# Neighbourhood attention: two places for pieces in a step, first scores among the projections, right output halves among the last steps

## The chip, the cores and the metric

The kernel runs on one core of a Trainium2 chip. Its time is that of one execution on the device, in microseconds (us). The engines of a core run beside each other, each in its own fixed order, and wait for each other by semaphores: TensorE (PE) multiplies and transposes, VectorE (DVE), ScalarE (ACT) and GpSimd (POOL) work on tiles, and SyncE (SP) issues most of the DMA transfers. PE writes to banks of PSUM, which the other engines read and so release.

## What is computed

Two layers of a diffusion backbone on 128 prompt tokens and 1024 latent tokens of width 1024. Layer 0 projects each token into a convolution module and eight heads of attention, each with a SiLU gate, and projects the joined results back; layer 1 is a pooling mixer. The change lies in the attention of layer 0 and in the start of its output projection.

```python
q = rms_norm(q, q_norm); k = rms_norm(k, k_norm)          # 8 heads of 64
# prompt: plain softmax attention of 128 tokens
# latent: each query sees a window of 8 rows x 16 columns, and all 128 cached keys
s_win = q . k_window * 64**-0.5 + rpb      # blocks of 16 columns: 8 rows x 32 keys, masked
s_ctx = q . k_ctx * 64**-0.5
p = softmax(concat(s_win, s_ctx)); y_att = p . concat(v_window, v_ctx)
z = concat(y_conv * silu(ga), y_att * silu(gb));  y = x + gate * (z @ w_out)
```

## The kernel before

All products are made in float32 by splitting both factors into a high and a low part and adding three matmuls. Projections run in chains of 24 matmuls (L232) for a group of 384 tokens (three groups, g) and 128 output columns; the last stage of them, `p_ga`, makes the gate of the convolution, four chains for each group. Ahead of the attention it calls `attention_ahead(g)`, which lays down the bias of the first pair of heads, the first pair's q and k (`prep`) and its values.

The attention is a list of 16 steps: four pairs of heads, two halves of the tokens (hf), two pairs of column blocks (j0). The functions in a step are

- `scores`: twelve matmuls (L877) into four banks of the kind "mm". Four times DVE adds the bias and takes the maximum (L885), ACT takes the exponential (L892), DVE the reciprocal (L896), and POOL scales p (L898). `p` stands in tiles of the kind `whi`, which also hold split weights.
- `turn`: four transposes of p (L904) into a bank of the kind "tp" or "cv" (there are two of each), four turns a step. ACT copies three of the banks to `pt` (L1033, L1038), DVE the last (L1039).
- `values`: 32 matmuls (L913) into a "cv" bank, and DVE multiplies the gate in (L924).
- pieces. `prep` of the next pair has five: two halves of q (L813), two halves of k (L820), each four transposes whose high part ACT writes (L804) and whose low part DVE writes (L805); and `rest` (L832 to L834), three transposes with two copies to `qc` on ACT, the high part of the cached keys on ACT (L840), the low part on DVE and two copies on POOL. `prompt_attention` has four: scores (L938) with DVE's maxima and scale (L940, L941) and two exps on ACT (L943); the scaling by POOL (L948); two transposes and a copy (L953, L954); the values (L959).

The order on PE, ACT and DVE in the attention is the order of the code, written out in `attention_steps` by hand; the order on POOL and SP is set by a scheduler when the kernel is built and is then as fixed. In the loop for s the scores of step s + 1 come first, then the values of step s - 1, then the turns of step s. The pieces come at the end of a step:

```python
            prompt[i]()
            for piece in pieces[2 * i : 2 * i + 2]:
                later.append(piece())
```

i is s % 4. All of them take "cv" banks (the prompt's parts also "tp"), and DVE's part of a piece, `later`, runs at the start of the next step. The first scores, of steps 0 and 1, come after the last projection.

After the attention `out0` projects nine tiles of 128 tokens: `out_right` and `out_left` are 24 matmuls each (L1101, L1094), for 512 of 1024 columns. Right weights are loaded and split by `load_right` (L1063 on SP, two buffers; L1073 on POOL, L1074 on DVE) among the last four steps. Left weights are two units, loaded at L204, split by ACT (L186) and DVE (L187); the layer's gates come by four loads (L408), x by y loads (L1118), z is split by L1085 and L1086.

Of the kernel before, what the change touches and what calls it, by code (L numbers as in the profile page):

```python
# [46 lines left out]
def _body(tc, nc, A, O, const, wp, arena, tmpp, smp, psp):  # L47
# [736 lines left out]
    def v_load(pr):  # L784
        vw = {}
        for jj in range(2):
            t = slot(VS[pr % 2][jj], name="vw")[:, :1280].rearrange("p (x c) -> p x c", c=P)
# [9 lines left out]
    def prep(pr):  # L797
# [9 lines left out]
        def q_half(i):  # L807
            if i == 0:
                st["q"] = [slot(x, F32R, "q")[:, :D] for x in QS[pr % 2]]
            b = bank("cv")  # L810
# [6 lines left out]
        def k_half(i):  # L817
            b = bank("cv")
            for t in range(4):
                te.transpose(out=b[:, t * P : (t + 1) * P], in_=qk_at(4 * i + t, pr)[:, P : 2 * P], identity=ident)  # L820
            if i == 0:

                st["k"] = [slot(x, F32R, "k") if x is not None else gr_tile(F32R)[:, :SLOT] for x in KS[pr % 2]]
# [3 lines left out]
        def rest():  # L827
# [3 lines left out]
            b = bank("cv")  # L831
# [3 lines left out]
            se.activation(qc[:, 0:P], b[:, 0:P], AF.Copy, scale=qn8)  # L835
            se.activation(qc[:, P : 2 * P], b[:, P : 2 * P], AF.Copy, scale=kn)
# [13 lines left out]
        return [lambda: q_half(0), lambda: q_half(1), lambda: k_half(0), lambda: k_half(1), rest]  # L850
# [11 lines left out]
    def scores(step, mem=None):  # L862
# [7 lines left out]
        def matmuls(i):  # L870
# [7 lines left out]
            if mem is not None:  # L878
                ps.append(mem[:, i * 1024 : (i + 1) * 1024].rearrange("p (e k) -> p e k", e=2))
            else:  # L880
                ps.append(wp.tile([P, 2, 512], F32, tag="whi", bufs=4, name=nm("p")))
# [47 lines left out]
    def prompt_attention(pr):  # L929
# [5 lines left out]
        def first():  # L935
# [9 lines left out]
        def second():  # L945
            ve.reciprocal(st[:, 6:8], st[:, 4:6])
            for e in range(2):
                gp.tensor_scalar(pp[:, e * P : (e + 1) * P], pp[:, e * P : (e + 1) * P], st[:, 6 + e : 7 + e], 0.0, ALU.mult, ALU.add)  # L948

        def third():  # L950
            tb = bank("tp")
            for e in range(2):
                te.transpose(out=tb[:, e * P : (e + 1) * P], in_=pp[:, e * P : (e + 1) * P], identity=ident)  # L953
            se.copy(pp[:, 2 * P : 4 * P], tb[:, : 2 * P])  # L954

        def fourth():
            ob = bank("cv")
# [6 lines left out]
            ve.tensor_tensor(zv, ob[:, :P], zv, ALU.mult)  # L964

        return first, second, third, fourth
# [3 lines left out]
    def attention_ahead(g):  # L970
# [4 lines left out]
        elif g == 1:  # L975
            for piece in prep(0):
                piece()()
            with tc.issue_after(last["ck"]):
                hold["V"] = v_load(0)
        else:  # L980
            bias_init(1)
            bias_load(0, 1)

    def attention():
        nonlocal gr
        first = hold["S"] = scores(STEPS[0], gr_tile())
        for i in range(2):
            first[0](i)
            for e in range(2):
                first[1](i, e)  # L990
            first[2](i)
# [3 lines left out]
        gr = gr_tile()  # L995

    def attention_steps():


        n = len(STEPS)  # L1000
        sc_, vw, pts = {0: hold["S"]}, {0: hold["V"]}, {}
        pieces, later, right = [], [], None
        for s in range(n + 1):
            i, pr = s % 4, s // 4
            while later:
                later.pop(0)()
            nxt = None
            if s + 1 < n:
# [3 lines left out]
                nxt[1](0, 0)  # L1012
                nxt[1](0, 1)
                nxt[1](1, 0)
# [12 lines left out]
            ps = sc_.pop(s)[3]  # L1027
            pt = pts[s] = [wp.tile([P, 2, 512], F32, tag="wlo", bufs=4, name=nm("pt")) for _ in range(2)]
# [5 lines left out]
            if nxt:  # L1034
                nxt[1](1, 1)
            tb = bank("tp")
# [5 lines left out]
            prompt[i]()  # L1042
            for piece in pieces[2 * i : 2 * i + 2]:
                later.append(piece())
            if i == 2 and pr < 3:
                vw[pr + 1] = v_load(pr + 1)
            if pr == 3:
                if i == 0:
                    right = load_right(0, (13, 15, 17, 2, 3, 4))
                hold["R"] = next(right)  # L1050


    def load_right(l, ids, ahead=2):
# [11 lines left out]
        for k0 in range(0, 2 * ahead, 2):  # L1065
            load(k0)
        for k0 in range(0, 8, 2):
# [11 lines left out]
    def zsplit(zt, t, ids):  # L1079
# [3 lines left out]
        for kh in range(2):  # L1083
            src = zt[g, kh][:, :, a : a + P]
            se.copy(hi[:, 4 * kh : 4 * kh + 4, :], src)  # L1085
            ve.tensor_tensor(lo[:, 4 * kh : 4 * kh + 4, :], src, f(hi[:, 4 * kh : 4 * kh + 4, :]), ALU.subtract)  # L1086
        return hi, lo

# [23 lines left out]

    def out0(WL, WR, gate):
        zt = {(g, kh): (zc, za)[kh][g] for g in range(3) for kh in range(2)}
        xn = []
        for t in range(9):
            y = slot((0, 1, 8, 9)[t % 4], name="y")[:, :D]
            sy.dma_start(y, x_src(t))  # L1118
            zs = zsplit(zt, t, ((5, 16), (6, 7))[t % 2])
            c = 1 if t == 8 else 0  # L1120
            add_gated(y, out_right(zs, WR), 1, gate[c, 1])
# [158 lines left out]
    def go_out0():  # L1280
        gate = load_gates(0)
        out0(hold["L0"] + hold["L1"], hold["R"], gate)
# [65 lines left out]
```

## Time and profile before

| | us |
|---|---|
| median of 3 runs | 996.78 (994.22 to 997.67) |
| profiled execution | 996.42 |
| its span in the profile | 994.6 |
| PE busy in the span | 951.6 |
| DVE, ACT, POOL busy | 599.2, 408.3, 366.9 |

The profile is of one execution, and its span is 1.8 us shorter than the execution's time. A bracket behind a row of the timeline is idle time of that engine ahead of the row and what ended it. Ends of matmuls are modelled, so the distance of two starts tells more than a matmul's own length.

### The profile page before, as it was taken

Reading aid. Unit: us, or ns where it says so; the run is one execution under the profiler, and the core shown is the slowest. Engines: PE = TensorE matmul, PEld = TensorE weight load, DVE = VectorE, ACT = ScalarE, POOL = GpSimd, SP = SyncE. Lnnn points to the kernel's source line nnn. Section 1 sums busy time; section 2 is a strip of 40 time slices with the busy share of each in tenths; the row PEclk is TensorE's granted clock in tenths of the full one; section 3 lists DMA queues with packets and bytes.
Section 4 is the critical chain, followed back from the end, with each engine's and each line's share of the span. In section 5 each row is a group of like instructions: output and inputs, shape, how many; then the busy total and the mean of one; then the engine's idle time right before and its main releaser. Section 6 shows DMA issues by size and latency. Waiting matters only on the chain.

```text
span 994.6 us, 16662 instructions
## 1 busy us (share of the span) xinstructions
PE 951.6 (96%) x6388; PEld 865.3 (87%) x6388; DVE 599.2 (60%) x1231; ACT 408.3 (41%) x827; POOL 366.9 (37%) x485
## 2 busy tenths in 40 slices
PE   5888999999999999998898899999999999999998
PEld 3686988899999999986677788889999999998887
DVE  3567999999763344456677556475435545585332
ACT  3375666765411244247777423335212222231010
POOL 2264888998743301024445245351000000004322
PEclk9998999999999999999999999999999999999999
DMA  9969654226111111133433612151101111133311
GB/s 299 337 196 288 233 172 146 87 86 234 46 46 46 46 43 43 37 85 111 114 103 97 212 65 105 44 200 48 41 29 43 53 43 54 64 106 101 132 64 65
DMA packets 87531, 108.54 MB, mean 109 GB/s; under 512 B 10700, under 2 KB 73036, under 8 KB 87339
## 3 DMA queue, kind: packets, MB, share of 16 engines
q1 hardware_dynamic: 82539, 95.93, 30.5%
q0 software_dynamic: 2576, 9.18, 2.4%
q10 hardware_dynamic: 2336, 2.36, 0.7%
q8 instruction: 50, 0.82, 0.3%
q14 instruction: 30, 0.25, 0.1%
HBM read 94.64 MB, written 21.57 MB: 117 GB/s over the span
## 4 chain that ended last, share of the span: by engine, by line
PE 83%; DMA 5%; DVE 4%; ACT 3%; SPq 3%; issue 2%; POOL 1%; DVEq 0%; POOLq 0%; ACTq 0%
PE mm L232 39%; PE mm L239 16%; PE mm L1101 10%; PE mm L1094 9%; PE mm L1246 2%; PE tp L342 2%; ACT p L892 2%; SPq L757 2%; DMA raw<-in_w_out 1%; DVE p L885 1%; DMA bias<-texp 1%; PE mm L877 1%; DMA wad<-in_w_ada 1%; DMA raw<-in_w_in 1%; PE tp L904 1%
## 5 line engine op out<-in xcount | busy, mean ns | idle before, releaser
L232 PE MATMUL mm<-h,whi 128*128 128x384 f32 x1536 | 399.0, 339 | 2.7 <-ACT whi L186 1.8
L232 PEld LDWEIGHTS mm<-h,whi 128*128 128x128 f32 x1536 | 278.1, 189 | 10.0 <-ACT gr L474 2.6
L232 PE MATMUL mm<-h,wlo 128*128 128x384 f32 x768 | 258.7, 338 | 0.3 <-DVE wlo L187 0.3
L476 POOL TENSOR_TENSOR zc<-zc,gr 128x384 f32<-128x384 f32 x138 | 150.5, 1092 | 30.9 <-ACT gr L474 21.9
L239 PE MATMUL mm<-whi,h 128*128 128x256 f32 x864 | 157.1, 284 | 0.0
L232 PEld LDWEIGHTS mm<-h,wlo 128*128 128x128 f32 x768 | 145.4, 189 | 1.3 <-issue 0.7
L239 PEld LDWEIGHTS mm<-whi,h 128*128 128x128 f32 x864 | 135.1, 192 | 3.9 <-ACT gr L474 2.6
L239 PE MATMUL mm<-wlo,h 128*128 128x256 f32 x432 | 122.2, 283 | 0.0
L187 DVE TENSOR_TENSOR wlo<-raw,whi 128x1024 fp32r<-128x1024 f32 (+1 forms) x56 | 69.3, 1237 | 55.0 <-ACT whi L186 54.7
L487 DVE SCALAR_TENSOR_TENSOR cv<-u,convw,cv 128x384 f32<-128x384 f32 (+2 forms) x208 | 95.0, 511 | 0.9
L1094 PE MATMUL mm<-whi,zs 128*128 128x512 f32 (+1 forms) x304 | 92.8, 379 | 2.0 <-ACT whi L186 2.0
L1101 PE MATMUL mm<-wrh,zs 128*128 128x512 f32 x288 | 92.4, 391 | 0.4 <-POOL wrh L1073 0.4
L186 ACT CAST whi<-raw 128x1024 fp32r<-128x1024 f32 (+1 forms) x56 | 56.9, 1017 | 70.3 <-PE mm L232 23.6
L239 PEld LDWEIGHTS mm<-wlo,h 128*128 128x128 f32 x432 | 82.9, 192 | 0.0
L1108 POOL TENSOR_TENSOR y<-y,og 128x512 f32<-128x512 f32 x34 | 48.7, 1434 | 86.6 <-DVE og L1106 83.4
L474 ACT ACTIVATE gr<-u,convw 128x384 f32<-128x384 f32 (+2 forms) x128 | 64.3, 531 | 30.8 <-POOL zc L476 30.3
L1094 PEld LDWEIGHTS mm<-whi,zs 128*128 128x128 f32 x304 | 56.0, 188 | 12.7 <-ACT whi L186 2.2
L1101 PEld LDWEIGHTS mm<-wrh,zs 128*128 128x128 f32 x288 | 53.9, 188 | 11.9 <-POOL wrh L1073 0.8
L898 POOL TENSOR_SCALAR p<-p,st 128x512 f32<-128x512 f32 x60 | 44.3, 752 | 53.0 <-DVE st L896 45.3
L1106 DVE TENSOR_TENSOR og<-mm,gr 128x512 f32<-128x512 f32 x34 | 23.3, 687 | 57.7 <-PE mm L1101 33.4
L456 ACT ACTIVATE th<-mm 128x384 f32<-128x384 f32 x48 | 23.5, 489 | 83.1 <-PE mm L232 83.0
L1094 PE MATMUL mm<-wlo,zs 128*128 128x512 f32 (+1 forms) x152 | 57.3, 378 | 0.0
(216 smaller groups left out, 1380.2 us busy)
## 6 DMA issues: line engine op xcount, KB each, us to landing
raw<-in_w_in SPq DMA_DIRECT2D x28, 512.0 KB
wad<-in_w_ada SPq DMA_DIRECT2D x16, 768.0 KB
wada<-in_w_ada SPq DMA_DIRECT2D x16, 512.0 KB
raw<-in_w_in SPq DMA_DIRECT2D x32, 256.0 KB
raw<-in_w_out SPq DMA_DIRECT2D x16, 512.0 KB
vw<-vwin SPq DMA_DIRECT2D x8, 640.0 KB
y0scr<-y POOLq DMA_DIRECT2D x9, 512.0 KB, 3.2
y<-y0scr SPq DMA_DIRECT2D x9, 512.0 KB
```

Of the source, the lines that this page charges most:

```text
L186: se.copy(hi[:, :n], raw[:, :n])
L187: ve.tensor_tensor(lo[:, :n], raw[:, :n], f(hi[:, :n]), ALU.subtract)
L232: te.matmul(out, wsl(units, a, k, c0, P), hsl(hs, b, k, g), start=(k == 0 and i == 0), stop=(k == nk - 1 and i == 2))
L239: te.matmul(out, hsl(hs, p, k, g, a, P), wsl(units, q, k, 0, 256), start=(k == 0 and i == 0), stop=(k == 7 and i == 2))
L456: se.activation(th[:, :n], ps, AF.Tanh, scale=0.5)
L474: se.activation(pr[:, o : o + n], src, AF.Copy, scale=w)
L476: gp.tensor_tensor(z, z, pr, ALU.add)
L487: ve.scalar_tensor_tensor(zp if k == 30 else acc, src, convw[:, c, k : k + 1], zp if k == NPTS[c] else acc, ALU.mult, ALU.add)
L898: gp.tensor_scalar(ps[i][:, e, :], ps[i][:, e, :], st[:, 4 + e : 5 + e], 0.0, ALU.mult, ALU.add)
L1094: te.matmul(b[:, c0 : c0 + n], zs[p][:, k, :], WL[k // 2][q][:, k % 2, c0 : c0 + n], start=(k == 0 and i == 0), stop=(k == 7 and i == 2))
L1101: te.matmul(b, zs[p][:, k, :], WR[q][k // 3][:, k % 3, :], start=(k == 0 and i == 0), stop=(k == 7 and i == 2))
L1108: gp.tensor_tensor(yv, yv, t, ALU.add)
```

## The change

Three parts. First, the scores of step 0 are made in `p_ga`, ahead of the last projection chain (g = 2, i = 2); their p is in `whi` tiles instead of a tile of its own. The bias of the second half, the values of even pairs and the keys of odd pairs get other slots; the second bias is laid down one group earlier.

Second, each step has two places for pieces: a, with a "cv" bank, between the next step's scores and the values, and b, with a "tp" bank, ahead of the last turn. The place a piece gets:

| i | a | b |
|---|---|---|
| 0 | q, first half | q, second half |
| 1 | k, first half | k, second half |
| 2 | rest | prompt: scores |
| 3 | prompt: transposes | prompt: values |

DVE's part of a piece runs after the four reduces of the same step. The prompt's scaling joins its first piece, so there are three. `rest` copies to `qc` on DVE instead of ACT, and so does the prompt's copy. In the last pair, which has no `prep`, the prompt's three pieces stand at a in steps 12, 13 and 14.

Third, the right weights start one step earlier; the gates' loads and the first two y loads come in step 13, the raw loads of the first left unit and a part of z's split in step 14, the rest of the split of two tiles in step 15. `out_right` of tile 0 stands in step 15 between the values and the turns, that of tile 1 behind them, ahead of the last values.

```diff
+                if g == 2 and i == 2:
+                    first_scores()
             attention_ahead(g)
...
-    BS = ((0, 1), (8, 9))
+    BS = ((0, 1), (6, 7))
     QS = ((2, 3), (10, 11))
-    KS = ((4, 5), (None, 12))
-    VS = ((6, 7), (14, 16))
+    KS = ((4, 5), (9, 12))
+    VS = ((None, 8), (14, 16))
...
-            se.activation(qc[:, 0:P], b[:, 0:P], AF.Copy, scale=qn8)
-            se.activation(qc[:, P : 2 * P], b[:, P : 2 * P], AF.Copy, scale=kn)
...
+                ve.tensor_scalar(qc[:, 0:P], b[:, 0:P], qn8, None, ALU.mult)
+                ve.tensor_scalar(qc[:, P : 2 * P], b[:, P : 2 * P], kn, None, ALU.mult)
...
+    def first_scores():
+
+        mm, ex, norm, ps = hold["S"] = scores(STEPS[0])
+        for i in range(2):
+            mm(i)
+            for e in range(2):
+                ex(i, e)
+            norm(i)
...
+                ab = ([*prompt, None], [None] * 4) if last_ else ((pieces[0], pieces[2], pieces[4], prompt[1]), (pieces[1], pieces[3], prompt[0], prompt[2]))
+            if s == n - 2:
+                zs_part(0, 0)
+            if s == n - 1:
+                zs_part(0, 1)
+                zs_part(1, 0)
+                zs_part(1, 1)
+            if s == n:
+                out0_ahead(1)
+                units[L0_AT] = [split(*r) for r in raws[L0_AT]]
+            if nxt:
+                nxt[1](0, 0)
+            a = ab[0][i]("cv") if s < n and ab[0][i] else None
             gate = values(STEPS[s - 1], pts.pop(s - 1), vw[STEPS[s - 1][0]]) if s else None
+            if nxt:
+                nxt[1](0, 1)
+                nxt[1](1, 0)
+            if a:
+                a()
             if nxt:
                 nxt[2](0)
             if gate:
                 gate()
+            if s == n - 1:
+                out0_ahead(0)
...
+            b = ab[1][i]("tp") if ab[1][i] else None
             tb = bank("tp")
             turn(tb, ps[1][:, 1, :])
...
-            if pr == 3:
-                if i == 0:
-                    right = load_right(0, (13, 15, 17, 2, 3, 4))
+            if n - 6 <= s < n - 1:
                 hold["R"] = next(right)
+            if s == n - 3:
+                gr = gr_tile()
+                hold["gate"] = load_gates(0)
+                y_of(0)
+                y_of(1)
+            if s == n - 2:
+                raws[L0_AT] = load_raw(items[L0_AT][0])
```

On PE, around the prompt's transposes of the first pair, before, at the end of a third step (`tp` and `cv` are banks, `p` scaled scores, `pp` the prompt's p, the numbers are buffers):

```order
L904 MATMUL tp_5244<-ident,p_5093 128x128 x4
L904 MATMUL tp_5245<-ident,p_5093 128x128 x4
L904 MATMUL cv_5246<-ident,p_5105 128x128 x4
L904 MATMUL tp_5262<-ident,p_5105 128x128 x4
L953 MATMUL tp_5272<-ident,pp_5025 128x128 x2
L832 MATMUL cv_5278<-ident,qk_2995 128x128
L833 MATMUL cv_5278<-ident,qk_2995 128x128
L834 MATMUL cv_5278<-ident,qc_5276 128x128
L877 MATMUL mm_5292<-gr_5172,q_5069 128x512
```

And now, in the fourth step, behind the scores of the step that follows:

```order
L879 MATMUL mm_5302<-k_5107,q_5027 128x512
L954 MATMUL cv_5314<-ident,pp_5023 128x128 x2
L912 MATMUL cv_5317<-pt_5243,gr_4831 64x128 x8
L912 MATMUL cv_5317<-pt_5244,gr_4831 64x128 x8
L903 MATMUL tp_5344<-ident,p_5180 128x128 x4
L903 MATMUL tp_5345<-ident,p_5180 128x128 x4
L903 MATMUL cv_5346<-ident,p_5192 128x128 x4
L960 MATMUL tp_5362<-pp_5023,VP 64x128 x2
L903 MATMUL tp_5365<-ident,p_5192 128x128 x4
```

The transposes (L953, now L954) have gone from behind the turns of a third step to ahead of the values of a fourth, with the prompt's values (L960) ahead of the last turn of the same step.

On ACT in the scores of step 13, made in step 12, before (`p_6191` and `p_6203` are the two tiles of these scores, `pp_6210` is the last prompt's p):

```order
L892 ACTIVATE p_6191,st_6192<-p_6191,st_6192 128x512 x2
L892 ACTIVATE p_6203,st_6204<-p_6203,st_6204 128x512
L1033 COPY pt_6234<-tp_6236 128x512
L1033 COPY pt_6234<-tp_6237 128x512
L892 ACTIVATE p_6203,st_6204<-p_6203,st_6204 128x512
L1038 COPY pt_6235<-cv_6238 128x512
L943 ACTIVATE pp_6210,st_6211<-cv_6264,st_6211 128x128
L943 ACTIVATE pp_6210,st_6211<-tp_6265,st_6211 128x128
```

And now:

```order
L891 ACTIVATE p_6208,st_6209<-p_6208,st_6209 128x512
L942 ACTIVATE pp_6224,st_6225<-cv_6227,st_6225 128x128
L942 ACTIVATE pp_6224,st_6225<-tp_6228,st_6225 128x128
L891 ACTIVATE p_6208,st_6209<-p_6208,st_6209 128x512
L891 ACTIVATE p_6220,st_6221<-p_6220,st_6221 128x512
L1055 COPY pt_6263<-tp_6265 128x512
L1055 COPY pt_6263<-tp_6266 128x512
L891 ACTIVATE p_6220,st_6221<-p_6220,st_6221 128x512
L1061 COPY pt_6264<-cv_6267 128x512
```

The prompt's two exps (L943, now L942) have moved from the end of the step to a place between the first two of the four exps.

On POOL in the last steps, before (`wrh` are the high parts of right weights):

```order
L898 TENSOR_SCALAR p_6191<-p_6191,st_6192 128x512 x2
L898 TENSOR_SCALAR p_6203<-p_6203,st_6204 128x512 x2
L898 TENSOR_SCALAR p_6297<-p_6297,st_6298 128x512 x2
L1073 TENSOR_SCALAR wrh_6274<-raw_6287 128x512 x2
L898 TENSOR_SCALAR p_6309<-p_6309,st_6310 128x512 x2
L948 TENSOR_SCALAR pp_6210<-pp_6210,st_6211 128x128 x2
```

And now, with the end of the third pair ahead of it:

```order
L897 TENSOR_SCALAR p_5988<-p_5988,st_5989 128x512 x2
L897 TENSOR_SCALAR p_6000<-p_6000,st_6001 128x512 x2
L947 TENSOR_SCALAR pp_5812<-pp_5812,st_5813 128x128 x2
L897 TENSOR_SCALAR p_6115<-p_6115,st_6116 128x512 x2
L897 TENSOR_SCALAR p_6127<-p_6127,st_6128 128x512 x2
L1101 TENSOR_SCALAR wrh_6098<-raw_6198 128x512 x2
L947 TENSOR_SCALAR pp_6224<-pp_6224,st_6225 128x128 x2
L897 TENSOR_SCALAR p_6208<-p_6208,st_6209 128x512 x2
L897 TENSOR_SCALAR p_6220<-p_6220,st_6221 128x512 x2
```

The scaling of the third pair's prompt (`pp_5812`) stands behind both p of that step; the last prompt's (`pp_6224`) has come ahead of p of its step, and a part of the right weights stands ahead of both.

## Rows read from the trace of the kernel before

**Rows 1.** Window: length; busy us of PE, PEld, DVE, ACT, POOL; clock; DMA share, GB/s

```profile
475.00:500.00 25.00, 21.79 (x228) 17.14 (x225) 16.60 (x54) 18.88 (x50) 9.65 (x16) 1.00 0.32 92
```

**Rows 2.** The chain of waits: start, length, what; entry and tail

```profile
432.92 7.13 PE mm L232 x41
...
553.75 5.34 DMA raw<-in_w_out
559.17 1.05 ACT whi L186
...
571.68 10.20 PE mm L1094 x45
...
582.56 4.99 PE mm L1101 x22
```

**Rows 3.** Timeline of PE at the entry: start, length, line, tiles, idle before

```profile
447.83 0.63 PE L904 MATMUL tp<-ident,gr 128*128 128x128 f32 x4 [0.83 <-ACT pt L1033]
...
451.26 1.69 PE L877 MATMUL mm<-k,q 64*128 64x512 f32 x12
```

**Rows 4.** Timeline of PE in the second and third round

```profile
480.86 0.50 PE L877 MATMUL mm<-gr,q 64*128 64x512 f32 x2
...
487.65 0.66 PE L820 MATMUL cv<-ident,qk 128*128 128x128 f32 x4 [0.51 <-ACT pt L1038]
488.24 0.51 PE L877 MATMUL mm<-gr,q 64*128 64x512 f32 x2
...
489.86 1.97 PE L913 MATMUL cv<-pt,vw 128*64 128x128 f32 x32
491.76 1.09 PE L904 MATMUL tp<-ident,p 128*128 128x128 f32 x8
...
493.79 0.41 PE L953 MATMUL tp<-ident,pp 128*128 128x128 f32 x2
494.03 0.27 PE L832 MATMUL cv<-ident,qk 128*128 128x128 f32 x1
...
495.94 1.91 PE L877 MATMUL mm<-k,q 64*128 64x512 f32 x12 [1.42 <-ACT k L840]
...
501.72 0.44 PE L959 MATMUL cv<-pp,VP 128*64 128x128 f32 x4
502.09 1.69 PE L877 MATMUL mm<-k,q 64*128 64x512 f32 x12
```

**Rows 5.** Timeline of PE in the last steps

```profile
531.89 0.51 PE L877 MATMUL mm<-gr,q 64*128 64x512 f32 x2
...
543.80 0.63 PE L904 MATMUL tp<-ident,p 128*128 128x128 f32 x4 [1.08 <-POOL p L898]
...
550.74 0.63 PE L904 MATMUL tp<-ident,p 128*128 128x128 f32 x4 [0.88 <-POOL p L898]
...
552.08 1.97 PE L913 MATMUL cv<-pt,vw 128*64 128x128 f32 x32
...
560.27 0.50 PE L1094 MATMUL mm<-whi,zs 128*128 128x512 f32 x1 [1.95 <-ACT whi L186]
```

**Rows 6.** Timelines of DVE, ACT and POOL in the attention

```profile
478.83 0.27 DVE L940 TENSOR_REDUCE st<-cv 128x1 f32<-128x128 f32 x1
...
489.74 0.68 DVE L885 CUSTOM_DVE_ANT_0 p<-mm,bias 128x512 f32<-128x512 f32 x1
...
479.76 0.37 ACT L943 ACTIVATE pp<-cv,st 128x128 f32<-128x128 f32 x1 [0.74 <-DVE st L941]
...
489.01 0.73 POOL L948 TENSOR_SCALAR pp<-pp,st 128x128 f32<-128x128 f32 x2
...
494.90 1.36 POOL L898 TENSOR_SCALAR p<-p,st 128x512 f32<-128x512 f32 x2 [1.02 <-DVE st L896]
...
545.52 2.32 POOL L898 TENSOR_SCALAR p<-p,st 128x512 f32<-128x512 f32 x2
```

**Rows 7.** Timeline of the SP queue: the gates' loads

```profile
547.24 1.82 SPq L408 DMA_DIRECT2D gr<-gsc  x4
```

More of the change, by code (lines that the diff above doesn't have):

```diff
@@ L821, in k_half, with rest @@
             if i == 0:
-                st["k"] = [slot(x, F32R, "k") if x is not None else gr_tile(F32R)[:, :SLOT] for x in KS[pr % 2]]
+                st["k"] = [slot(x, F32R, "k") for x in KS[pr % 2]]
             o = slice(256 + i * 512, 768 + i * 512)
             return two_parts(b, st["k"][0][:, o], st["k"][1][:, o], kn)
-        def rest():
+        def rest(tag):
             qc = tmp("qc")
@@ L860, in za_tok, with scores @@
         return out
-    def scores(step, mem=None):
+    def scores(step):
         pr, hf, j0 = step
@@ L877, in matmuls @@
                     te.matmul(bs[e].rearrange("p (r c) -> p r c", c=32), q[H[e], qo], kv, start=(n == 0), stop=(n == 2))
[L878 to L881, printed above, removed]
+            ps.append(wp.tile([P, 2, 512], F32, tag="whi", bufs=4, name=nm("p")))
             sts.append(small(8, "st"))
@@ L943, in first, with later, second, third @@
                 se.activation(pp[:, e * P : (e + 1) * P], bs[e][:, :P], AF.Exp, bias=st[:, 2 + e : 3 + e], accum_out=st[:, 4 + e : 5 + e])
[L945 to L951, printed above, removed]
+            def later():
+                ve.reciprocal(st[:, 6:8], st[:, 4:6])
+                for e in range(2):
+                    gp.tensor_scalar(pp[:, e * P : (e + 1) * P], pp[:, e * P : (e + 1) * P], st[:, 6 + e : 7 + e], 0.0, ALU.mult, ALU.add)
+            return later
+        def second(tag):
+            tb = bank(tag)
             for e in range(2):
                 te.transpose(out=tb[:, e * P : (e + 1) * P], in_=pp[:, e * P : (e + 1) * P], identity=ident)
-            se.copy(pp[:, 2 * P : 4 * P], tb[:, : 2 * P])
-        def fourth():
-            ob = bank("cv")
+            return lambda: ve.tensor_copy(pp[:, 2 * P : 4 * P], tb[:, : 2 * P])
+        def third(tag):
+            ob = bank(tag)
             for e in range(2):
@@ L963, in fourth @@
             zv = za[2][:, pr, 256:384]
-            ve.tensor_tensor(zv, ob[:, :P], zv, ALU.mult)
-        return first, second, third, fourth
+            return lambda: ve.tensor_tensor(zv, ob[:, :P], zv, ALU.mult)
+        return first, second, third
     STEPS = [(pr, hf, j0) for pr in range(4) for hf in range(2) for j0 in (0, 2)]
@@ L976, in attention_ahead, with new_pt @@
             for piece in prep(0):
-                piece()()
+                piece("cv")()
+            bias_init(1)
+            bias_load(0, 1)
             with tc.issue_after(last["ck"]):
                 hold["V"] = v_load(0)
-        else:
-            bias_init(1)
-            bias_load(0, 1)
-    def attention():
[L985 to L991, printed above, removed]
+    def first_scores():
+        mm, ex, norm, ps = hold["S"] = scores(STEPS[0])
+        for i in range(2):
+            mm(i)
+            for e in range(2):
+                ex(i, e)
+            norm(i)
+    def new_pt():
+        return [wp.tile([P, 2, 512], F32, tag="wlo", bufs=4, name=nm("pt")) for _ in range(2)]
+    def attention():
         E = mybir.EngineType
@@ L994, in attention @@
             attention_steps()
-        gr = gr_tile()
     def attention_steps():
+        nonlocal gr
         n = len(STEPS)
         sc_, vw, pts = {0: hold["S"]}, {0: hold["V"]}, {}
-        pieces, later, right = [], [], None
+        right = load_right(0, (13, 15, 17, 2, 3, 4))
         for s in range(n + 1):
             i, pr = s % 4, s // 4
-            while later:
-                later.pop(0)()
+            last_ = pr == 3
             nxt = None
@@ L1027, in attention_steps @@
             ps = sc_.pop(s)[3]
-            pt = pts[s] = [wp.tile([P, 2, 512], F32, tag="wlo", bufs=4, name=nm("pt")) for _ in range(2)]
+            pt = pts[s] = new_pt()
             tbs = [bank("tp"), bank("tp"), bank("cv")]
@@ L1041, in attention_steps @@
                 nxt[2](1)
-            prompt[i]()
-            for piece in pieces[2 * i : 2 * i + 2]:
-                later.append(piece())
+            if b:
+                b()
             if i == 2 and pr < 3:
                 vw[pr + 1] = v_load(pr + 1)
-            if pr == 3:
-                if i == 0:
-                    right = load_right(0, (13, 15, 17, 2, 3, 4))
+            if n - 6 <= s < n - 1:
                 hold["R"] = next(right)
+            if s == n - 3:
[5 more added lines that the diff above has]
+                raws[L0_AT] = load_raw(items[L0_AT][0])
     def load_right(l, ids, ahead=2):
@@ L1280, in go_out0 @@
     def go_out0():
-        gate = load_gates(0)
-        out0(hold["L0"] + hold["L1"], hold["R"], gate)
+        out0(hold["L0"] + hold["L1"], hold["R"], hold["gate"])
     items.append(([A["w_out_0"][512:1024, 0:512]], keep("L1", go_out0)))
```

52 lines of the change are left out of this document (33 added, 19 removed).

## The prediction

> **What bounds the kernel now.** I read the windows first, then the timeline of PE, then the other engines where PE waits. In the attention no engine is full by its busy time except PE [rows 1]: of 25 us PE shows 21.79, ACT 18.88, DVE 16.60, POOL 9.65, at a granted clock of 1.00. The reader should see that the stage is close to PE's limit, with the others loaded enough to be late. The timeline of PE then gives where it is not. A step is PE's unit here: scores of the next step, values of the step before, four turns of this one. Its slots stand in [rows 4]: 488.24 to 489.86 scores, 1.62; to 491.76 values, 1.90; to 493.79 the 16 transposes of the turns, 2.03; together 5.55. Four steps, a pair of heads, are one round: scores start at 451.26 and at 480.86 in the same place of the round [rows 3, 4], so a round takes 29.60. Its extra pieces are four halves of q and k at 0.50 each (a quarter of 2.03, the same sixteen transposes), the rest at 0.33, the prompt's scores 0.40, its transposes 0.24 (493.79 to 494.03) and its values 0.37 (501.72 to 502.09). So 4 x 5.55 + 2.00 + 1.34 = 25.54 is PE's own work, and 4.06 of each round is waiting. The largest single wait is 1.42, where the scores want the k that ACT writes after the piece "rest" [rows 4]; one of 0.51 stands ahead of a half whose bank a copy on ACT still holds, and like ones elsewhere.
>
> The second loss is at the entry: the first scores run after the last projections with nothing beside them, and a wait of 0.83 and smaller ones stand there [rows 3]. The third is the tail [rows 5]: waits of 1.08, 0.88 and 1.95, the last for the output weights, whose load was issued at 553.75 and split at 559.17 [rows 2].
>
> **The change part by part.** I set each engine's instructions down in the changed order and gave each the slot of a like row, starting when its engine, inputs and bank are free. The order of before treated in that way gives a round of 29.46 against 29.60, so 0.14 a round is the error of the method where the waits are known.
>
> Entry. The last chain is 24 of the 41 matmuls of 7.13 us [rows 2], 4.17 us, so it starts at 440.05 - 4.17 = 435.88, and 451.26 comes 15.4 later. After: scores(0) 1.62; the chain waits for a bank until the first reduce on DVE is done, 0.8 (a reduce takes 0.68, [rows 6], and its start lags the matmuls' end); chain 4.17; scores(1) 1.62 with 0.3 for a bank of the chain; three turns 1.48 and two halves 1.00, the last turn 0.55; a wait of 1.5 before the second half, whose bank is freed by a copy on ACT that stands behind the exps. That is 12.9, so **-2.5**. If the bank wait is as long as all four reduces, 2.7, a gain of 0.6 is left; without the waits of 0.8 and 0.3 it is 3.6.
>
> Rounds. With two places the bank of a piece is released in the step itself. A half at each of two places costs its 0.50, and the wait for "rest" is gone, since k is written most of a step before the scores that want it. Steps with k halves: 5.55 + 1.00 + 0.1 = 6.65; with the rest and the prompt's scores: 5.55 + 0.73 + 0.05 = 6.33; with q halves 6.45. The fourth step has a new wait. Its piece at place a is the prompt's two transposes (0.24), which read what POOL has scaled, and in POOL's row that stands behind both scalings of the step's own p. The prompt's scores end 5.7 into the third step; DVE's maxima and scale take 0.93 (478.83 to 479.76), ACT's two exps about 0.72 (two of 0.37, [rows 6]), so the scaling could start at 7.5. POOL does the step's two p first, 1.36 from 7.75 on when their exps release them, then two pp in 0.73 [rows 6], and ends at 9.8. PE arrives at 6.33 + 1.62 = 7.95 and waits 1.9. The values and turns that stand behind it on PE wait as well, and ACT's copies of the turns. The step is 5.55 + 0.24 + 0.37 + 1.94 = 8.10. A round is 6.65 + 6.33 + 8.10 + 6.45 = 27.5, **2.1 less**. No row of before shows this wait: it could be 0, if the scaling of the prompt got in first, or 2.9, if the two p take 2.32 as beside the split of the right weights [rows 6]. I take 1.9 since all its terms have rows. From 451.26 to 531.89 there are two rounds and three steps: before 80.63, after 27.5 + 27.5 + 6.65 + 6.33 + 8.10 = 76.1, **-4.5**.
>
> The moved copies (two scalings and a prompt copy from ACT to DVE) I cost at nothing: DVE is idle for 8.4 of 25 [rows 1], and the copies stand behind the reduces, where nothing is due at once. Without that cover each delays a bank by about the 0.37 of a like tile on ACT [rows 6], some 3 us for the nine of them. The bias loads stand as far ahead of their reduces as before, and DVE has no idle time put down to them.
>
> Last pair. Step 12 has the prompt's scores at place a. On ACT its two exps now stand between the first and second exp of the next scores, so ACT must wait for DVE's maxima, which stand behind four reduces and two pieces of the right weights' split. One tp bank is held so long; the second turn waits 2.2 for it and the last turn 1.0 for a copy behind the delayed exps. The step is 5.55 + 0.40 + 3.05 = 9.0. The next two are 5.55 + 0.24 + 0.33 and 5.55 + 0.37 + 0.2, 6.1 each. Sum 21.2 for 531.89 to 552.08, which was 20.19 with the waits 1.08 and 0.88 in it [rows 5]: **+1.0**. Without the hold in step 12 it would be -2.0; with POOL's p at 2.32 in that step, +2.0.
>
> Tail. From the start of values(14) to the end of two right output halves PE has 1.90 + 5.45 + 2.03 + 5.45 + 1.90 = 16.7 (24 matmuls at 4.99/22 = 0.227, [rows 2]). Before it was 552.08 to 571.68 less three left matmuls that were done by then, 0.68: 18.9. The 1.95 wait is covered by the right halves, **-2.2**. What is late next are the weights of the second left unit: two loads (5.34 to land, [rows 2]), two casts of 1.05 and their low parts. In my listing they are ready 1.9 before they are wanted; what goes beyond that comes on the end.
>
> Gates and y are loaded earlier on the SP queue; they stand ahead of two loads of right weights there, see below. The sum: -2.5 - 4.5 + 1.0 - 2.2 = -8.2. The profiled execution took 996.42, so 988.2; it lies 0.36 under the median of the runs, so 988.6 against the median. I predict **988.5**.
>
> **The rivals.** First, the new wait in the fourth steps is not there: 1.94 in each of three. For it: the wait is the difference of sums over three engines. Against: POOL's order is fixed, with p first. It gives 988.5 - 5.8 = 982.7.
>
> Second, the steps become bound by the other engines. A shorter round puts the same work of ACT, 18.88 x 29.6 / 25 = 22.4 us [rows 1], into 27.5, 81%, and each piece's bank now waits inside the step for ACT and DVE in turn. With 0.4 more of that in each of 15 steps, a size like the 0.51 of before [rows 4], 6 us of the gain go: 994.5. For it: each wait that I took away came from a bank behind a copy. Against: ACT and DVE each keep 5 us to spare in a round.
>
> Third, and slower than before: the right weights come late. On SP four gate loads, 1.82 us of issue [rows 7], which wait for PE to be done with the tile that they fill, now stand ahead of the loads of the third and fourth part of the right weights. POOL's copy of each part stands in its row ahead of p of that step and of the prompt's scaling, and PE's turns wait for these. I have the load issued 2.3 into step 12 and wanted 9.9 into it, so 7.6 are free; the longest landing in the rows is 5.34 [rows 2]. From a landing of 7.6 us on, each us costs 1 in each of the two parts. To end slower than 999.8 both must eat 11.3 together, that is land after 7.6 + 5.7 = 13.3 us each; at 15 us each it is 988.5 + 14.8 = 1003.3.
>
> Fourth, the first and last parts of the change don't do what they say: scores(0) ahead of the last chain only make the chain wait, and the right halves push the left halves' weights back by as much. That loses 2.5 and 2.2: 993.2.
>
> Fifth, PE has room inside its slots: the pieces at two places go beside the matmuls around them and cost PE nothing. That is 3.34 less a round for 2.75 rounds, 9.2: 979.3. For it: weight loads are busy for 17.14 of the 25 us in which PE shows 21.79 [rows 1], so 31% of the window is free of them. Against: the slots of [rows 4] follow each other without a gap and still make 5.55. [...]
>
> **How the numbers follow.** A difference under 0.3%, 3.0 us, can't be told from none here: faster means below 993.8. The forecast, with sizes off by up to 0.2 in a step, 985.5 to 991.5, has 0.58; the first rival 0.15; the second 0.12, a third of it under 993.8; the third 0.05, slower; the fourth 0.08, half of it under 993.8; the fifth 0.02. Faster is 0.58 + 0.15 + 0.04 + 0.04 + 0.02 = 0.83, slower 0.05, same 0.04 + 0.08 = 0.12. The range goes from the first rival to halfway into the second, 982.5 to 994.0; it leaves out the third and the fifth, most of the second and the low end of the first, near 0.2.
>
> **What would show it.** Scores starts spaced by 6.4 to 6.7, 6.3 and 8.1; PE idle about 1.9 before the prompt's transposes in each fourth step, put down to POOL's pp; about 9 for step 12; the first looped scores at 448.8; no 1.95 before the output phase. It is wrong if the fourth steps are like the others, if PE idles in the k or q steps for ACT's copies, or if POOL waits for the right weights' raw tiles.

## The result and the profile after

The changed kernel takes 989.17 us in the median (988.84 to 989.89, 4 runs), the kernel before beside it 996.10 (994.22 to 997.67, 4 runs). The ratio is 0.9932, 95% interval 0.9913 to 0.9952: faster by 6.9 us, and the forecast was 988.5. The profiled execution took 989.12 us with a span of 987.4, against 996.42 and 994.6.

The same window as in [rows 1], of the changed kernel, with the same columns:

```profile
475.00:500.00 25.00, 23.85 (x251) 18.55 (x250) 18.68 (x62) 18.86 (x49) 11.10 (x18) 1.00 0.36 106
```

PE is busy for 23.85 of 25 instead of 21.79; ACT has kept its 18.9, DVE has taken 2.1 more. The timeline of PE over the first round answers [rows 4]. Each score group (L879) with its start is the beginning of a step:

```profile
454.32 1.69 PE L879 MATMUL mm<-k,q 64*128 64x512 f32 x12
...
460.85 1.69 PE L879 MATMUL mm<-k,q 64*128 64x512 f32 x12
463.66 0.68 PE L954 MATMUL cv<-ident,pp 128*128 128x128 f32 x2 [1.12 <-POOL pp L947]
464.27 1.97 PE L912 MATMUL cv<-pt,gr 128*64 128x128 f32 x32
...
468.62 1.70 PE L879 MATMUL mm<-k,q 64*128 64x512 f32 x12
...
475.27 1.68 PE L879 MATMUL mm<-k,q 64*128 64x512 f32 x12
...
481.89 1.69 PE L879 MATMUL mm<-k,q 64*128 64x512 f32 x12
```

From 454.32 to 481.89 a round takes 27.57; it was 29.60. The wait of 1.42 for k is gone, and in the fourth step PE waits 1.12 for the prompt's scaling, which is the new wait of the prediction. POOL's rows show why:

```profile
461.89 1.37 POOL L897 TENSOR_SCALAR p<-p,st 128x512 f32<-128x512 f32 x2 [1.11 <-PE mm L879]
463.23 0.73 POOL L947 TENSOR_SCALAR pp<-pp,st 128x128 f32<-128x128 f32 x2
```

The prompt's p (L947) comes behind the step's own p (L897). The entry, which answers [rows 3]:

```profile
434.26 2.21 PE L879 MATMUL mm<-k,q 64*128 64x512 f32 x12
436.70 0.62 PE L232 MATMUL mm<-h,whi 128*128 128x384 f32 x2 [0.23 <-DVE st L884]
...
446.58 0.66 PE L816 MATMUL tp<-ident,qk 128*128 128x128 f32 x4 [1.34 <-ACT pt L1055]
...
447.71 1.69 PE L879 MATMUL mm<-k,q 64*128 64x512 f32 x12
```

And the last steps with the tail, which answer [rows 5]:

```profile
523.75 1.70 PE L879 MATMUL mm<-k,q 64*128 64x512 f32 x12
...
530.03 0.63 PE L903 MATMUL tp<-ident,p 128*128 128x128 f32 x4 [1.89 <-ACT pp L942]
...
531.91 0.85 PE L903 MATMUL tp<-ident,p 128*128 128x128 f32 x4 [0.81 <-ACT pt L1055]
532.69 2.93 PE L879 MATMUL mm<-k,q 64*128 64x512 f32 x12
...
539.86 1.69 PE L879 MATMUL mm<-k,q 64*128 64x512 f32 x12
...
545.63 0.63 PE L903 MATMUL cv<-ident,p 128*128 128x128 f32 x4 [0.95 <-DVE st L895]
...
546.63 1.97 PE L912 MATMUL cv<-pt,vw 128*64 128x128 f32 x32
...
563.45 0.50 PE L1125 MATMUL mm<-whi,zs 128*128 128x512 f32 x1
```

Step 12 takes 8.94 with the two waits that were foreseen. The scores behind it take 2.93 instead of 1.7, which was not. ACT shows that the hold of 1.89 is the foreseen one: the prompt's exps wait there for DVE's scale, which stands behind the split of the right weights and the four reduces.

```profile
529.08 0.37 ACT L942 ACTIVATE pp<-cv,st 128x128 f32<-128x128 f32 x1 [1.62 <-DVE st L940]
```

In the kernel before, the last chain and the left halves begin here:

```profile
435.71 0.51 PE L232 MATMUL mm<-h,whi 128*128 128x384 f32 x2
...
571.51 0.62 PE L1094 MATMUL mm<-whi,zs 128*128 128x512 f32 x2
```

The sum by stretch, from the two traces, by starts of matmuls (the prediction's 15.4 and 18.9 begin or end at modelled ends, 435.88 and 571.68):

| stretch | before | after | change | forecast |
|---|---|---|---|---|
| start of the attention's entry to scores(2) | 15.55 | 13.45 | -2.1 | -2.5 |
| scores(2) to scores(13) | 80.63 | 76.04 | -4.6 | -4.5 |
| scores(13) to values(14) | 20.19 | 22.88 | +2.7 | +1.0 |
| values(14) to the end of two right halves | 18.75 | 16.82 | -1.9 | -2.2 |
| sum | | | -5.9 | -8.2 |

The other 1.4 of the 7.3 us between the two profiled executions lies ahead of the change: the long block of projections starts at 204.31 in the trace after, and in three executions of the kernel before at 205.84, 203.51 and 204.11. It moves between executions of the same kernel, so not with the change. In all, 33 executions of the kernel before beside the experiments lie between 992.9 and 1000.4; part of that scatter arises in the attention, shown below.

### The profile page after: what moved, and what is told of

It is laid out like the page before. It is cut to its first block, busy times and chain, and to the rows that moved or that the text cites. A ratio compares the mean times of both kernels' runs of the same rounds, so it can differ in the third digit from the quotient of the medians.

```text
span 987.4 us, 16652 instructions
## 1 busy us (share of the span) xinstructions
PE 949.5 (96%) x6388; PEld 863.0 (87%) x6388; DVE 603.0 (61%) x1243; ACT 404.9 (41%) x815; POOL 368.4 (37%) x485
## 3 DMA queue, kind: packets, MB, share of 16 engines
q0 software_dynamic: 2576, 9.18, 2.4%
## 4 chain that ended last, share of the span: by engine, by line
PE 88%; DMA 7%; SPq 2%; DVE 1%; ACT 1%; issue 1%; POOL 1%; DVEq 0%; ACTq 0%; POOLq 0%
PE mm L232 37%; PE mm L239 16%; PE mm L1132 10%; PE mm L1125 10%; PE cv L912 3%; PE tp L903 2%; DMA wada<-in_w_ada 2%; PE mm L879 2%; PE mm L1295 2%; DMA tbias<-in_rpb 2%; PE tp L342 2%; DMA vwin<-in_cache_v 1%; DMA wad<-in_w_ada 1%; DMA raw<-in_w_out 1%; DMA raw<-in_w_in 1%; PE cv L903 1%
## 5 line engine op out<-in xcount | busy, mean ns | idle before, releaser
L897 POOL TENSOR_SCALAR p<-p,st 128x512 f32<-128x512 f32 x64 | 48.5, 771 | 49.6 <-DVE st L895 33.7
```

The lines of the kernel that those rows point to most:

```text
L897: gp.tensor_scalar(ps[i][:, e, :], ps[i][:, e, :], st[:, 4 + e : 5 + e], 0.0, ALU.mult, ALU.add)
```

## The experiments

Where two runs differ by a few us, their stretches in the trace are compared, since the beginning of an execution alone varies by up to 3.8: over all profiles here the block of projections starts at 203.51 to 207.27. Steps are measured from one group of scores to the next.

### Each part undone

**First scores behind the last chain.**

```diff
-                if g == 2 and i == 2:
+                if g == 2 and i == 3:
                     first_scores()
```

> The scores of step 0 stand behind the last projection chain again, all else as changed. Theory (they fill waits of the entry): the time from the start of that chain to the scores of step 2 goes from 13.45 in the changed kernel to between 14.5 and the 15.4 of the kernel before, so 990.3 to 991.1 against 989.2. Rival (the chain only waits instead): 13.4 to 13.6 and 989.2.

Measured: 990.06 (989.36 to 990.63). The stretch from the start of the chain to scores(2) is 13.75 against 13.45, so 0.3 and not 1.1 to 2.0; the median is 0.9 longer, with overlapping runs. The chain and the scores only change places, as the rival had it, and PE waits 0.58 and 1.26 there instead of 0.23 and 1.34. Most of the 2.1 us that the entry has lost came with the pieces: from scores(0) to scores(2) this run takes 9.50 and the kernel before 11.30, and what has left that stretch are the prompt's scores and the waits behind them. The run with the old places, below, shows the same from the other side.

**Right halves behind the last values.**

```diff
             if s == n:
-                out0_ahead(1)
                 units[L0_AT] = [split(*r) for r in raws[L0_AT]]
...
-            if s == n - 1:
-                out0_ahead(0)
             if s == n:
+                out0_ahead(0)
+                out0_ahead(1)
                 break
```

> Both right output halves stand behind the last values again, the rest as changed. Theory (they cover the copies and scalings of the last two steps): the stretch from values(14) to the end of both halves goes from 16.8 to 18.0 to 18.9, so 990.4 to 991.3. Rival (the weights of the left halves would have been waited for anyway, and the halves are pushed on to them): the left halves come without a wait and the time stays at 989.2.

Measured: 989.65 (988.92 to 990.03). From values(14) to the first left matmul 18.09 instead of 16.82: 1.27 more, the theory's lower end. The median is nevertheless only 0.5 above that of the changed kernel, because the same steps 12 and 13, ahead of the edit, took 8.72 and 6.10 here and 8.94 and 7.17 there. That is the clock, which stayed at 1.00 here and fell to 0.50 there, see below.

**Pieces in the old places.**

```diff
-((pieces[0], pieces[2], pieces[4], prompt[1]), (pieces[1], pieces[3], prompt[0], prompt[2]))
+([None] * 4, [None] * 4)
...
+            if pr < 3:
+                if i == 0:
+                    held = prompt[0]("tp")
...
+                for piece in pieces[2 * i : 2 * i + 2]:
+                    later.append(piece("cv"))
```

> The pieces of the first three pairs and their prompts stand at the end of a step as before, DVE's part of a piece at the start of the next step; the last pair, the first scores and the output halves as changed. Theory (two places take the waits away): a round goes from 27.55 to 29.0 to 29.6, in all +4 to +5.5, 993.3 to 994.7. Rival (the gain of the rounds comes from the copies that went from ACT to DVE): about +1, 990.

Measured: 995.04 (990.87 to 997.84, 10 runs), ratio to before 0.9977 (0.9960 to 0.9995). A round takes 28.80, less than the 29.60 of before: the wait for k is 0.63 here and 1.42 there, with the same places. What differs in a round are the copies on DVE. So both readings have a share: the places 1.23 a round, the copies 0.80. The entry is in this run too, with scores(0) ahead of the last chain and the pieces in the old places:

```profile
437.28 2.21 PE L879 MATMUL mm<-k,q 64*128 64x512 f32 x12
...
453.18 2.93 PE L879 MATMUL mm<-k,q 64*128 64x512 f32 x12
```

It takes 15.90 from scores(0) to scores(2), where the changed kernel takes 13.45 and the kernel before, from the start of its last chain, 15.55. Some 0.5 of it is a lower clock (0.50 from 451 to 456, see below), since its two halves of q take 2.38 to the next scores and 1.86 in the kernel before. So moving the scores of step 0 forward brings next to nothing without the two places.

**The copies alone, on the kernel before.**

```diff
-            se.activation(qc[:, 0:P], b[:, 0:P], AF.Copy, scale=qn8)
-            se.activation(qc[:, P : 2 * P], b[:, P : 2 * P], AF.Copy, scale=kn)
...
                 ve.tensor_tensor(lv, cx, f(hv), ALU.subtract)
+                ve.tensor_scalar(qc[:, 0:P], b[:, 0:P], qn8, None, ALU.mult)
+                ve.tensor_scalar(qc[:, P : 2 * P], b[:, P : 2 * P], kn, None, ALU.mult)
...
-            se.copy(pp[:, 2 * P : 4 * P], tb[:, : 2 * P])
+            ve.tensor_copy(pp[:, 2 * P : 4 * P], tb[:, : 2 * P])
```

> The kernel before with one part of the change alone: the two scalings of rest and the prompt's copy on DVE instead of ACT. Theory (these copies were on PE's path, since the high part of the cached keys stands behind them on ACT and the scores wait for it): the wait of 1.42 in each round falls to about 0.63, a round from 29.60 to 28.8, -2.4 in all. Rival, as in the prediction (they are hidden): 29.60 and no change.

The rows are the scores of step 8 in this run and of step 4 in the one above:

```profile
493.73 1.44 PE L877 MATMUL mm<-k,q 64*128 64x512 f32 x8 [0.63 <-ACT k L838]
```

```profile
469.27 1.91 PE L879 MATMUL mm<-k,q 64*128 64x512 f32 x12 [0.63 <-ACT k L840]
```

A round takes 28.81, as expected, and in its trace scores(15) comes 2.4 earlier after the entry's start. The times do not show it: 995.02 (990.58 to 997.51, 10 runs) against 994.68, ratio 0.9999 (0.9980 to 1.0018). With executions that scatter by 7 us this stays open; that the wait shrinks is shown, that the kernel as a whole gains from this part alone is not.

**The copies back on ACT, in the changed kernel.** The same lines the other way round, of which one:

```diff
-            return lambda: ve.tensor_copy(pp[:, 2 * P : 4 * P], tb[:, : 2 * P])
+            se.copy(pp[:, 2 * P : 4 * P], tb[:, : 2 * P])
```

> The two scalings of rest and the prompt's copy stand on ACT again, all else as changed. Theory A, as in the prediction (hidden on either engine): the rounds stay at 27.55, 989.2. Theory B (ACT is late in these steps; with the old places the wait for k had been 0.63 against 1.42 by the move alone): each round grows by 0.4 to 0.8, in all +1.2 to +2.4, about 991.

Measured: 991.35 (990.66 to 992.03). A round takes 27.84 instead of 27.57, all of it in the step with the rest: 6.82 instead of 6.53. That is 0.8 in three rounds, between theory A and B. The median is 2.2 above the changed kernel's, as theory B had it, but the profiled executions differ by 1.7, and 0.9 of that lies ahead of the attention; so the trace's 0.8 is what is shown. The four rounds side by side: old places 29.60 with the copies on ACT and 28.81 on DVE, two places 27.84 and 27.57. The places bring 1.76 or 1.24, the copies 0.79 or 0.27: they share the same wait.

### The new waits

**The prompt's scaling first.**

```diff
+            if b and i == 2:
+                b()
             if nxt:
                 nxt[2](1)
-            if b:
+            if b and i != 2:
                 b()
```

> In the third step of a round the prompt's scaling stands ahead of the second p on DVE and POOL, all else as changed. Theory (the wait of 1.12 in each fourth step is POOL's order): that wait falls under 0.3 and the step from 7.77 to about 6.9, no other step grows; three rounds give -2.5 to -3.3, so about 986.3. Rival (the scaling is late because the prompt's exps are late on ACT): the wait stays at about 1.1 and the time at 989.2.

Measured: 987.73 (985.53 to 988.67). The wait is gone, the fourth step takes 6.79 instead of 7.77 and no other has grown:

```profile
463.15 0.72 POOL L947 TENSOR_SCALAR pp<-pp,st 128x128 f32<-128x128 f32 x2 [1.42 <-DVE st L895]
463.84 0.69 POOL L897 TENSOR_SCALAR p<-p,st 128x512 f32<-128x512 f32 x1
```

The scaling now starts at 463.15 on POOL and p follows; PE's transposes start at 463.58 without a bracket. Three steps of 0.98 are 2.9. The order on POOL was the cause. The median has come down by 1.4 only, not to the 986.3 of the theory; the 2.9 is that of the steps in the trace.

**The last pair's prompt at place b.**

```diff
-([*prompt, None], [None] * 4) if last_
+([None] * 4, [*prompt, None]) if last_
```

> In the last pair the prompt's three pieces stand at place b of steps 12, 13 and 14 instead of a. Theory (its exps ahead of the step's exps hold ACT and a bank, and the idle PE then gets half the clock): step 12 goes from 8.94 to about 6.1, step 13 from 7.17 to 6.1, no stretch at a clock of 0.50; 985.2. Rival 1 (POOL waits for the right weights in any case, and PE's turns for POOL): only about 1.5 is gained, 987.7. Rival 2 (the split of the right weights on DVE makes the hold): no change, 989.2.

Measured: 988.95 (987.96 to 990.12). Step 12 falls to 6.78, but 13 takes 7.27 and from scores(15) to values(14) it is 7.39, with new waits of 1.25 and 1.21. In the run with the right halves back, which had the pieces at a and a clock of 1.00, the three are 8.72, 6.10 and 6.46: the hold at the exps is gone from step 12, and as much has come back in the two steps behind it. From scores(13) to values(14) it is 21.44, against 21.28 in that run and 22.88 after, where the clock fell to 0.50; this run has 1.00 from 524 to 546. So the pieces' place gives nothing by itself at a clock of 1.00; the theory fell, and the time is the second rival's. The 1.44 against the trace after has the size of the first rival, but not its cause: POOL waits here for DVE, not for a load.

```profile
536.64 1.37 POOL L897 TENSOR_SCALAR p<-p,st 128x512 f32<-128x512 f32 x2 [1.51 <-DVE st L895]
```

DVE in step 12, which starts at 524.37:

```profile
525.35 1.28 DVE L1102 TENSOR_TENSOR wrl<-raw,wrh 128x512 fp32r<-128x512 f32 x2
526.54 0.69 DVE L884 CUSTOM_DVE_ANT_0 p<-mm,bias 128x512 f32<-128x512 f32 x1
```

The split of the right weights (L1102) stands ahead of the four reduces (L884), which start 2.17 into the step.

**The split behind the reduces.** With the pieces at b:

```diff
             if gate:
                 gate()
+            if n - 6 <= s < n - 1:
+                hold["R"] = next(right)
...
             if i == 2 and pr < 3:
                 vw[pr + 1] = v_load(pr + 1)
-            if n - 6 <= s < n - 1:
-                hold["R"] = next(right)
```

> The last pair's prompt pieces at b of steps 12 to 14, and DVE's and POOL's split of the right weights behind the four reduces of a step instead of ahead of them. Theory (with the pieces at b the rest of the delay is the split: DVE starts the reduces 1.3 to 1.7 late, POOL scales p behind a load): step 12 to 14 go from 6.8, 7.3 and 7.4 to 6.1 to 6.4 each, so 2 to 3 under the run with the pieces at b alone, 986.5. Rival (the waits come from the pieces themselves): 988.9 as that run.

Measured: 985.89 (985.48 to 986.13), and DVE in step 12, which starts at 524.07:

```profile
525.19 0.69 DVE L884 CUSTOM_DVE_ANT_0 p<-mm,bias 128x512 f32<-128x512 f32 x1
...
528.11 1.28 DVE L1102 TENSOR_TENSOR wrl<-raw,wrh 128x512 fp32r<-128x512 f32 x2
```

The reduces start 1.12 into the step, and steps 12 and 13 take 6.04 and 6.49. From scores(13) to values(14) it is 18.57: 2.9 less than with the pieces at b alone. So with the pieces at b the split ahead of the reduces was what made the exps, the copies and so the banks late. The edit does two things at once: it lets the reduces start earlier, and it takes L1102 away from beside two p on POOL, which take 1.37 here in step 12 and 2.44 in the run before. Their shares were not measured apart, and the split behind the reduces with the pieces at a was not run.

**All together, and a reorder of the entry.** The three edits above, and in step 0 the copies of the turns stand ahead of the exps of step 1 on ACT; then the same without that reorder. The reorder:

```diff
-            if nxt:
+            if nxt and s:
                 nxt[1](0, 1)
                 nxt[1](1, 0)
             if a:
                 a()
-            if nxt:
+            if nxt and s:
                 nxt[2](0)
...
+            if s == 0:
+                nxt[1](0, 1)
+                nxt[1](1, 0)
+                nxt[2](0)
             if nxt:
                 nxt[1](1, 1)
```

> All three together: the prompt's scaling ahead of the second p, the last pair's pieces at b, the split of the right weights behind the reduces; and in step 0 the copies of the turns ahead of the exps of step 1 on ACT, for the wait of 1.34 in front of the second half of q. Theory: -2.5 to -3.3, -3.5 to -4.5 and -1.0 to -1.3 against the changed kernel: 980.5 to 982. Rival (what one frees, the next waits for: ACT and DVE set the steps): not under 985.

> As the run with all together, without the reordering of ACT in step 0. Theory (what the reordering frees in step 0 the next step gives back): the first steps take 6.65 and 6.62 instead of 5.25 and 7.88, and the time is that run's, 982.9, within 0.5. Rival (the reordering gains its 1.34): 984.2.

Measured: 982.92 (980.93 to 983.70), ratio to before 0.9853 (0.9832 to 0.9874); without the reorder 983.82 (982.06 to 984.60), ratio 0.9877 (0.9853 to 0.9900). Both beat the changed kernel. The first lies between the theory's 982 and the rival's 985; the 983.82 of the second is nearer to the rival's 984.2 than to the theory, but 0.9 is within what the beginning of an execution varies by, and the traces decide. A round takes 26.58, the last pair 18.07. The reorder of step 0 frees its 1.34 there and loses it in the next step:

```profile
446.98 1.69 PE L879 MATMUL mm<-k,q 64*128 64x512 f32 x12
...
449.50 1.97 PE L912 MATMUL cv<-pt,gr 128*64 128x128 f32 x32 [0.25 <-ACT pt L1067]
...
453.01 0.63 PE L903 MATMUL cv<-ident,p 128*128 128x128 f32 x4 [0.52 <-DVE st L895]
```

Steps 5.25 and 7.88 with it, 6.66 and 6.61 without: 13.13 and 13.27, so 0.14 is gained and not 1.34. The exps that were put back are late for the scaling, and the turns wait for that.

### The clock

Windows of the changed kernel over the end of step 12 and the scores that follow; the clock is the third number from the right:

```profile
531.00:532.70 1.70, 0.89 (x7) 0.49 (x6) 0.17 (x1) 1.70 (x5) 1.70 (x4) 0.85 0.93 364
532.70:533.70 1.00, 1.00 (x5) 0.81 (x6) 0.90 (x3) 0.74 (x3) 0.34 (x2) 0.50 0.15 61
...
535.60:537.00 1.40, 1.40 (x24) 1.23 (x24) 1.40 (x5) 1.40 (x5) 0.30 (x1) 1.00 0.49 130
```

And of the run with the right halves back, whose instructions up to there are the same:

```profile
532.00:533.30 1.30, 0.58 (x6) 0.44 (x6) 0.00 (x0) 1.30 (x5) 1.30 (x3) 1.00 0.90 350
533.30:535.00 1.70, 1.70 (x14) 1.13 (x14) 1.61 (x4) 0.96 (x3) 1.48 (x3) 1.00 0.05 19
```

After the same waits of 1.89 and 0.81 the granted clock fell to 0.50 in the one execution, from 532.2 to 535.6, and stayed at 1.00 in the other. The traces of the kernels before and after hold these two values alone, 0.50 and 1.00; a number between is the mean of a window with both. At this place it fell in the profiled runs of the changed kernel, of the first scores put back and of the copies put back, and did not in those of the right halves put back and the scaling first. From scores(13) to values(14) the former take 22.88, 22.94 and 22.61, the latter 21.28 and 21.27: with the fall it is 1.3 to 1.7 us more. In the run with the old places it stayed at 1.00 there, behind waits of 1.52 and 0.81, but fell in the entry, behind waits of 1.37, 0.53 and 0.32, for some 7 us:

```profile
451.00:453.00 2.00, 1.68 (x8) 1.13 (x6) 0.50 (x2) 1.37 (x5) 1.18 (x2) 0.50 0.60 171
```

From scores(2) to scores(3) that run takes 9.18, where the kernel before takes 7.37: with the 0.5 ahead of scores(2) some 2.3 us.

The kernel before has waits of a like size in every round, so it was profiled twice more, unchanged.

> The kernel before, unchanged, once more under the profiler: 12 of its 33 runs beside these kernels had a granted clock of 0.990 or less and took 997 to 1000, the others 993 to 997. Theory (the waits of the entry or of the tail let the clock fall in some executions): where the mean clock is 0.990 or less, a stretch at 0.50 stands between 440 and 465 or behind 558. Rival: the difference lies in the loads of the first 100 us alone.

> The kernel before, unchanged, a further time, with the same two readings: a stretch at a clock of 0.50 in the attention where the mean clock is 0.990 or less (theory), or none there in any run (rival).

Measured: 993.46 and 996.37, both with a mean clock of 0.993. The first has 1.00 all through the attention. The second has two falls there, one at the entry (0.64 from 447 to 450) and one behind the wait for k:

```profile
494.94 2.79 PE L877 MATMUL mm<-k,q 64*128 64x512 f32 x12 [1.42 <-ACT k L840]
...
496.00:498.00 2.00, 2.00 (x14) 1.17 (x12) 1.42 (x5) 0.69 (x2) 0.00 (x1) 0.50 0.29 80
```

That step takes 7.68 instead of 6.14, and the first two steps of the entry 0.75 more. So part of the scatter of the kernel before arises behind its waits: a wait of 1.42 costs 1.42, and in one of these executions the step behind it took 1.5 more at 0.50. That the wait lets the clock fall is the author's reading; no run shows it apart, and the other five waits of 1.42 in these two traces have no fall behind them. The half of the theory that ties it to a mean clock of 0.990 or less was not put to the test, since neither execution had one. The mean does not tell of the falls: it is 0.993 with two of them and with none, since the first 110 us had a clock of 0.97 in the one and 0.94 in the other. What the rows show is a fall to 0.50 in one execution and 1.00 in another for the same instructions.

## Why the prediction was right, and where its terms were not

- **The total**: 989.17 against 988.5, in the range. The path itself gave 5.9 and not 8.2 in the two profiled executions, and 1.4 came from ahead of the change. So the nearness of the total is in part luck.
- **Rounds**: 76.04 against 76.1. The steps were put at 6.65, 6.33, 8.10 and 6.45 and measured 6.61 to 6.63, 6.53, 7.77 and 6.63 to 6.65. That 76.1 came out at 76.04 is luck: the errors cancel. The new wait was at the foreseen place, POOL's p first, with 1.12 instead of 1.94: the sum let PE wait for both of the two pp, and it starts when the first is done, and POOL came 0.2 earlier. It was 0.2 low in the step with the prompt's scores and in the step with the q halves, whose 6.45 lies under the 5.55 + 1.00 of its own terms.
- **The copies at nothing**: a mis-sized term. They stood on PE's path, 0.79 a round in the old places and 0.27 in the new. The steps of the sum were set down in the changed order, with the copies on DVE, so the sum held their gain while the text put it at nothing and gave it to the places.
- **The entry**: -2.1 against -2.5, for the wrong reason; its terms add up to 13.04 and not 12.9, so the sum itself gives -2.4. The step that failed is the one that lets scores(0) fill waits: undone, it costs 0.3, and with it kept and the old places the entry is as long as before. The gain is the pieces'. The fourth rival was right on that half and wrong on its price.
- **The last pair**: +2.7 against +1.0. With the clock at 1.00 it is 21.28, where 21.2 was forecast, with the holds of 1.89 and 0.81 for 2.2 and 1.0. What was missed is the clock, which fell to 0.50 behind them: 1.6. The forecast laid the hold on the exps' place, behind reduces and split, and the trace agrees for step 12; that moving the exps alone wins nothing, since the split then holds the two steps behind, was not foreseen.
- **The tail**: -1.9 against -2.2; undone, 1.27 come back and not 1.95, since the left weights are split earlier in either case and no wait for them is left. What comes back are mostly waits of 0.79 and 0.28, for a copy and for the gate.
- **The third rival**: POOL did wait 2.58 in step 12 for a load of right weights. That load was issued at 526.08, behind the split of the tile it overwrites, three us after the last gate load: the gates do not delay it. PE's turns waited for the prompt's exps, not for POOL, so the price was nothing here. The prediction had named this wait of POOL as a sign that it is wrong; the sign came, and it told nothing.
- **The fifth rival**: the share of the weight loads rose from 17.14 to 18.55 of 25 while PE's rose to 23.85. No median of these runs is under 982.9, the slots kept their 1.6 and 1.9, and a step with two halves takes 6.63 where 5.55 + 1.00 is 6.55, so the pieces cost PE their own time. The best version has 26.58 a round where PE's own work is 25.54: what is left to gain there by these slots is 1.04.

## What to carry to other kernels

When pieces are laid between the steps of a pipeline, write down for each engine what stands ahead of the instruction that PE waits for; here one line of order on POOL was worth 2.9 us, and the place of the split on DVE and POOL as much again. Undo each part of a change alone before crediting it: the part that looked like the entry's gain gave 0.3, and copies that seemed hidden gave 0.8 a round in the old places. Look at the clock behind a wait of PE as well: behind one of 1.42 it fell to 0.50 in one of two executions, and the step took 1.5 more than in the other.

## What was not expected of the hardware

- The clock fell to 0.50 for some 3 us behind a wait of 1.42, and behind 1.89 and 0.81 close together, in some executions and not in others of the same instructions, at 1.3 to 1.7 us each. In two entries it fell behind waits of 1.37 at most, for 0.75 us of loss in one and 2.3 in the other.
- Two p on POOL take 1.36 to 1.38 in the rounds, and 2.44 and 2.25 in the last steps beside L1102 on DVE (`wrl<-raw,wrh`); with L1102 moved away the first pair takes 1.37. What in the two makes POOL slower no run shows.
